# A layer norm that scales the residual in place, with ACT making the next inputs and rescaling the residual later

## The chip, the cores and the metric

The kernel runs on one core of one Trainium2 chip. The core has TensorE (PE in the profile, with its weight loads as PEld), VectorE (DVE), ScalarE (ACT), GpSimd (POOL) and SyncE (SP, which here only issues transfers). The metric is the device time of one execution in microseconds. All times are from the chip, and the profile is one execution seen by the hardware profiler.

## The reference

A trunk of two layers works on x of 512 positions by 1024 channels. Each layer has three sublayers: a half-step feed-forward network (FFN), a token mixer (Mamba-2 SSD in layer 0, differential attention in layer 1), and a second half-step FFN. Every sublayer ends in the same way, and the next one begins with a modulation:

```
y = sublayer(x * (1 + scale) + shift)
x = layer_norm(ALPHA * x + gate * y, g, b)      # mean and variance over 1024 channels
layer_norm(v) = (v - mean) * rsqrt(var + 1e-5) * g + b
```

So between two sublayers two things are made from the normalised value `n = (v - mean) * rsqrt(var + eps)`: the next sublayer's inputs `u = n*G + B`, where G and B join the norm's g, b with the next scale and shift, and the next residual `ALPHA*x = n*(ALPHA*g) + ALPHA*b`. All matrix products are float32 in the reference.

## The kernel before

**Numbers.** Each float32 operand of a product is split in a high part in fp32r and a low part, the rest. A product takes three matmuls: high by high, high by low, low by high (L162). The high part is made by ACT as a rounded copy, the low part by DVE as a subtraction (L119 and L120 for most weights, L449 and L450 for others, L149 and L150 for activations). The norm's outputs are split likewise in `uh` and `ul`.

**Layout.** Activations lie transposed, channels on the 128 partitions and the 512 positions along a row. The residual is one tile `resid` of 8 blocks (d = 0 to 7) of 128x512. Sublayers are counted n = 0 to 5: FFN, SSD, FFN, FFN, attention, FFN.

**The end of a sublayer** (`down_units`, class `LN`). The down projection is added into the residual block by block by DVE (`add_res`, L366). The last four (or six) blocks are done in two halves of 256 positions, so that the first half can be normalised while TensorE still works on the second. `stats` gets mean and variance by small matmuls, GpSimd raises the variance to the power -0.5 (L317), and matmuls with the identity spread the result over the partitions into a PSUM tile `rb`. DVE then subtracts the mean in place (L321). `normalize` does, for each half and each block d:

```
lt = res * G * rb            # DVE, L348, reads PSUM
uh = lt + B   (fp32r)        # ACT, L349
ul = (lt + B) - uh           # DVE, L350
```

and at the half's end ACT copies `rb` to an SBUF tile `rs` (L353). After both halves `residual` makes the next residual on GpSimd: for each d, `res = res * rs` (L359) and `res = res * lnag + lnab` (L360), all 512 positions at once. It is first used when the next sublayer adds to the residual.

**The start of the next sublayer.** Its first weights (tiles `wah`, `wal`) were split ahead, and its first products run on halves, so that TensorE starts with the first half of `uh` and `ul`. In the FFNs n = 2, 3 and 5 the first four of 22 tiles are plain products (gate and up, then SiLU L533, product L535). In their course DVE and ACT build sums of the input blocks (`input_forms`, L426 to L431). The remaining 18 tiles use a scheme with seven products of half size in place of eight (`seven`), whose weight sums and splits DVE and ACT make for each tile (L449, L450, L459). While a tile runs, DVE also does multiply-and-sum units of the modulation's projection (`ada_unit`, L180).

**What sets the order.** The code records operations for each engine, and a list scheduler of the language orders each engine's instructions by its own estimate of when they could run; each engine then executes its list strictly in order and waits on semaphores. Only SyncE's queue issues weight loads, into four buffers `raw`.

Of the kernel before, what the change touches and what calls it, by code (L numbers as in the profile page):

```python
# [9 lines left out]
F32 = mybir.dt.float32  # L10
# [36 lines left out]
def hybrid_trunk(tc, xT, cb, par, cst, adaw, wgu, wdn0, wdn1, wdn2, wdt, win, wso, wqk, wv, wao, dist_in, dtp, lam_in, out):  # L47
# [17 lines left out]
    def tmp(name="tmp"):  # L65
        return tp.tile([P, T], F32, tag="t", name=name)
# [193 lines left out]
    class LN:  # L260
# [63 lines left out]
        def normalize(self, a, b, rb):  # L324
            n = self.n
            if n == 5:
                for d in range(KT):
                    t = res[d][:, a:b]
                    nc.vector.scalar_tensor_tensor(
                        out=t, in0=t, scalar=pc(C_LNG + n * 8 + d), in1=rb, op0=ALU.mult, op1=ALU.mult  # L330
                    )
                    nc.scalar.activation(t, t, AF.Identity, bias=pc(C_LNB + n * 8 + d))
                    if d % 2:
                        nc.sync.dma_start(
                            out[(d - 1) * P : (d + 1) * P, a:b].rearrange("(e p) t -> p e t", e=2),
                            resid[:, d - 1 : d + 1, a:b],
                        )
                return
            if self.u is None:
                self.u = [  # L340
                    tuple(ap.tile([P, T], F32R, tag="u", name=x, bufs=2 * KT) for x in ("uh", "ul")) for _ in range(KT)
                ]
                self.rs = ap.tile([P, T], F32, tag="l", name="rs", bufs=3)
            for d in range(KT):
                G, B = lnG[n][:, d : d + 1], lnB[n][:, d : d + 1]
                t = tmp("lt")[:, a:b]
                uh, ul = self.u[d][0][:, a:b], self.u[d][1][:, a:b]
                nc.vector.scalar_tensor_tensor(out=t, in0=res[d][:, a:b], scalar=G, in1=rb, op0=ALU.mult, op1=ALU.mult)  # L348
                nc.scalar.activation(uh, t, AF.Identity, bias=B)  # L349
                nc.vector.scalar_tensor_tensor(  # L350
                    out=ul, in0=t, scalar=B, in1=uh.bitcast(F32), op0=ALU.add, op1=ALU.subtract
                )
            nc.scalar.activation(self.rs[:, a:b], rb, AF.Copy)  # L353

        def residual(self):
            n = self.n
            if n < 5:
                for d in range(KT):
                    nc.gpsimd.tensor_tensor(out=res[d], in0=res[d], in1=self.rs, op=ALU.mult)  # L359
                    nc.gpsimd.tensor_scalar(  # L360
                        out=res[d], in0=res[d], scalar1=lnag[n][:, d : d + 1],
                        scalar2=lnab[n][:, d : d + 1], op0=ALU.mult, op1=ALU.add,
                    )

    def add_res(d, pd, n, a, b):
        nc.vector.scalar_tensor_tensor(  # L366
# [135 lines left out]
    def ffn(n, stream=None, per=(0, 0), pre=None, first7=FT):  # L502
# [9 lines left out]
        for pi, nf in enumerate(FPARTS):  # L512
            hs = []
            open7 = None
            for _ in range(nf):
                if f >= first7:
                    g = seven(load(wgu[idx, f, 0]), load(wgu[idx, f, 1]), forms, hs)
                    next(g)
                    if open7 is not None:
                        next(open7, None)  # L520
                    next(g)
                    open7 = g
                    f += 1
# [12 lines left out]
                hs.append(split_act(h))  # L536
                if first7 - 4 <= f < first7:
                    making = making or input_forms(u)
                    forms.append(next(making))
                f += 1  # L540
                if f > 3 or n > 0:
                    advance(stream, per[0])

            if open7 is not None:
                next(open7, None)

            def mk(d):
# [20 lines left out]
    def ssm(n):  # L568
# [307 lines left out]
    def attention(n):  # L876
# [285 lines left out]
```

## Time and profile before

| | us |
|---|---|
| median of 3 runs | 2261.39 |
| lowest, highest | 2259.89, 2261.66 |
| the profiled execution | 2260.94 |
| its span | 2259.2 |
| PE, DVE, ACT, POOL busy | 2170.5, 1746.3, 989.0, 403.5 |
| mean granted TensorE clock | 0.988 |

The profiled execution's time is 1.7 us more than its span, which counts from the first instruction's start to the last one's end. A group's row gives the line, the engine, the operation, out<-in by tile names, the shape, the count, and then the busy time, the mean of one in ns and the idle time just before. A wait's row gives the waiting engine, tile and line, the releaser, the total in us, how many times, and the longest. A row of stretches gives the stretch, its length, the busy time and count for PE, PEld, DVE, ACT and POOL, the granted clock (1.00 is full), the share of the DMA engines and GB/s. The norms' ends lie at 380 to 400 us (n = 0), 833 to 851 (n = 1), 1209 to 1233 (n = 2), 1580 to 1603 (n = 3) and 1879 to 1900 (n = 4).

### The profile page before, as it was taken

What the parts mean: (1) busy time and instruction counts of PE and PEld (TensorE: products, weight loads), DVE (VectorE), ACT (ScalarE), POOL (GpSimd) and SP (SyncE); (2) the same over time, 40 slices, a digit from 0 to 9 for tenths busy, and PEclk for the clock granted to TensorE, in tenths of its full rate; (3) what the DMA queues carried; (4) which work ended last, traced back from release to release, by engine and by line L of the source; (5) the groups of instructions that cost most, each with busy time, mean ns of one, the idle gap of its engine ahead of it and who ended that gap; (6) DMA issues with size and microseconds to landing.
All of it is one profiled execution on the core that took longest, in us unless ns stands there. A gap on an engine that the chain in (4) does not pass through costs nothing.

```text
span 2259.2 us, 33641 instructions
## 1 busy us (share of the span) xinstructions
PE 2170.5 (96%) x13030; PEld 1866.5 (83%) x13030; DVE 1746.3 (77%) x2850; ACT 989.0 (44%) x1648; POOL 403.5 (18%) x412
## 2 busy tenths in 40 slices
PE   7999999999999988999999899999999999899998
PEld 5788889866777677898999889899877779889897
DVE  6864668656766689998888998897866679959696
ACT  4422234567656534343453334343555544425353
POOL 3000003344222335000014200003300025100003
PEclk9999999999999999999999999999999999999999
DMA  8864652564544413646442273633211111323231
GB/s 301 281 212 161 206 169 78 124 174 141 163 125 128 126 47 112 215 140 201 145 131 76 83 252 102 234 110 115 67 57 57 57 60 63 102 86 106 91 114 46
DMA packets 88545, 296.97 MB, mean 131 GB/s; under 512 B 9536, under 2 KB 12992, under 8 KB 88384
## 3 DMA queue, kind: packets, MB, share of 16 engines
q1 hardware_dynamic: 88384, 294.81, 40.9%
q8 instruction: 102, 1.67, 0.3%
q14 instruction: 59, 0.48, 0.1%
HBM read 289.53 MB, written 5.24 MB: 130 GB/s over the span
## 4 chain that ended last, share of the span: by engine, by line
PE 54%; DVE 17%; issue 5%; ACT 3%; DMA 2%; POOL 2%; POOLq 0%; ACTq 0%; DVEq 0%; SPq 0%
PE acc L162 42%; PE mid L162 5%; DVE wl L120 2%; DVE raw L459 2%; PE mid L782 2%; DVE lo L150 1%; DVE wl L450 1%; DMA raw<-in_wdn 1%; DVE ul L350 1%; DVE raw L180 1%; PE mid L931 1%; PE ln L162 1%; DVE lt L348 1%; ACT wh L119 1%; PE ln L249 1%
## 5 line engine op out<-in xcount | busy, mean ns | idle before, releaser
L162 PE MATMUL acc<-hi,wh 128*128 128x512 f32 (+1 forms) x1488 | 506.6, 341 | 20.0 <-ACT wh L449 10.0
L162 PE MATMUL acc<-hi,wl 128*128 128x512 f32 (+1 forms) x1488 | 505.9, 340 | 5.5 <-DVE wl L450 5.5
L162 PE MATMUL acc<-lo,wh 128*128 128x512 f32 (+1 forms) x1488 | 504.9, 340 | 0.0
L162 PE MATMUL acc<-uh,wh 128*128 128x512 f32 (+1 forms) x1256 | 442.6, 353 | 4.5 <-ACT px L482 4.4
L162 PE MATMUL acc<-ul,wh 128*128 128x512 f32 (+1 forms) x1256 | 439.7, 350 | 0.1
L162 PE MATMUL acc<-uh,wl 128*128 128x512 f32 (+1 forms) x1256 | 438.5, 350 | 1.3 <-DVE wl L120 1.3
L119 ACT ACTIVATE wh<-raw 128x1024 fp32r<-128x1024 f32 (+1 forms) x234 | 239.2, 1027 | 410.1 <-PE acc L162 212.1
L120 DVE TENSOR_TENSOR wl<-raw,wh 128x1024 fp32r<-128x1024 f32 (+1 forms) x234 | 288.0, 1232 | 86.5 <-ACT wh L119 77.5
L162 PEld LDWEIGHTS acc<-hi,wh 128*128 128x128 f32 x1488 | 283.5, 191 | 58.0 <-ACT wh L449 10.6
L162 PEld LDWEIGHTS acc<-hi,wl 128*128 128x128 f32 x1488 | 284.0, 191 | 37.0 <-DVE wl L450 6.3
L162 PEld LDWEIGHTS acc<-lo,wh 128*128 128x128 f32 x1488 | 283.8, 191 | 31.2 <-DVE lo L150 1.3
L162 PEld LDWEIGHTS acc<-uh,wh 128*128 128x128 f32 x1256 | 238.3, 190 | 45.1 <-issue 9.4
L162 PEld LDWEIGHTS acc<-uh,wl 128*128 128x128 f32 x1256 | 238.2, 190 | 35.9 <-issue 3.9
L162 PEld LDWEIGHTS acc<-ul,wh 128*128 128x128 f32 x1256 | 238.5, 190 | 33.8 <-issue 4.7
L449 ACT ACTIVATE wh<-raw 128x1024 fp32r<-128x1024 f32 x162 | 170.8, 1059 | 211.1 <-DVE raw L459 107.6
L180 DVE SCALAR_TENSOR_TENSOR raw<-raw,cond 128x1024 f32<-128x1024 f32 x144 | 179.5, 1254 | 52.4 <-DMA raw<-in_adaw 52.0
L450 DVE TENSOR_TENSOR wl<-raw,wh 128x1024 fp32r<-128x1024 f32 x162 | 197.0, 1220 | 28.6 <-ACT wh L449 27.7
L112 POOL TENSOR_TENSOR wal<-raw,wah 128x512 fp32r<-128x512 f32 x13 | 19.7, 1517 | 895.8 <-ACT wah L110 308.4
L366 DVE SCALAR_TENSOR_TENSOR resid<-acc,gv,resid 128x512 f32<-128x512 f32 (+1 forms) x172 | 113.0, 659 | 76.7 <-PE acc L162 76.2
L459 DVE TENSOR_TENSOR raw<-raw 128x512 f32<-128x512 f32 x216 | 150.3, 698 | 4.4
L162 PE MATMUL mid<-uh,wh 128*128 128x256 f32 (+2 forms) x332 | 94.8, 286 | 1.0 <-DVE up L491 0.9
L162 PE MATMUL mid<-uh,wl 128*128 128x256 f32 (+2 forms) x332 | 94.0, 284 | 0.6 <-DVE wl L120 0.6
(270 smaller groups left out, 3920.1 us busy)
## 6 DMA issues: line engine op xcount, KB each, us to landing
raw<-in_wgu SPq DMA_DIRECT2D x176, 512.0 KB, 3.9
raw<-in_adaw SPq DMA_DIRECT2D x144, 512.0 KB, 4.4
raw<-in_wdn SPq DMA_DIRECT2D x64, 448.0 KB, 3.5
raw<-in_win SPq DMA_DIRECT2D x40, 512.0 KB, 3.6
raw<-in_wdn SPq DMA_DIRECT2D x32, 512.0 KB, 4.6
rw<-scr SPq DMA_DIRECT2D x32, 512.0 KB, 5.6
ch<-scr SPq DMA_DIRECT2D x32, 256.0 KB, 3.6
raw<-in_wso SPq DMA_DIRECT2D x16, 512.0 KB, 3.4
```

Of the source, the lines that this page charges most:

```text
L119: nc.scalar.activation(hi[:, :n], raw, AF.Copy)
L120: nc.vector.tensor_tensor(out=lo[:, :n], in0=raw, in1=hi[:, :n].bitcast(F32), op=ALU.subtract)
L150: y = nc.vector.tensor_tensor(out=lo, in0=src, in1=hi.bitcast(F32), op=ALU.subtract)
L162: last = nc.tensor.matmul(o, lhsT=a, rhs=b, start=start and j == 0, stop=j == n - 1, skip_group_check=not start)
L180: nc.vector.scalar_tensor_tensor(out=raw, in0=raw, scalar=1.0, in1=cond, op0=ALU.mult, op1=ALU.mult, accum_out=mods[l][:, j : j + 1],)
L249: nc.tensor.matmul(o[:, j * P : (j + 1) * P], lhsT=cols[:, j : j + 1].broadcast_to([P, P]), rhs=ident, start=True, stop=True)
L348: nc.vector.scalar_tensor_tensor(out=t, in0=res[d][:, a:b], scalar=G, in1=rb, op0=ALU.mult, op1=ALU.mult)
L366: nc.vector.scalar_tensor_tensor(out=res[d][:, a:b], in0=pd[:, a:b], scalar=gvec[n][:, d : d + 1], in1=res[d][:, a:b], op0=ALU.mult, op1=A ...
L449: nc.scalar.activation(x[0], r, AF.Copy)
L450: nc.vector.tensor_tensor(out=x[1], in0=r, in1=x[0].bitcast(F32), op=ALU.subtract)
L459: nc.vector.tensor_tensor(out=o, in0=x, in1=y, op=ALU.add)
L782: nc.tensor.matmul(py[hh * 64 : (hh + 1) * 64, cc], lhsT=lhs, rhs=rhs, start=k == 0, stop=k == 2)
```

## The change

For the norms n = 0 to 4, `normalize` now multiplies the centred residual by `rb` in place on DVE, so that the residual block itself holds the normalised value. ACT makes `uh` from it with scale G and bias B, and a second time, unrounded, `lt`; DVE subtracts the two for `ul`. The tile `rs` and its copies are gone. `residual` issues nothing itself: it puts eight operations on a list `later`, each of which rescales one block (128x512) on ACT with scale and bias. They are issued by `scale_residual`: in an FFN two after each of the first four tiles, in the SSD after the first SiLUs, in the attention after the first value unit. The last norm, n = 5, is unchanged.

```diff
             if self.u is None:
                 self.u = [
                     tuple(ap.tile([P, T], F32R, tag="u", name=x, bufs=2 * KT) for x in ("uh", "ul")) for _ in range(KT)
                 ]
-                self.rs = ap.tile([P, T], F32, tag="l", name="rs", bufs=3)
             for d in range(KT):
                 G, B = lnG[n][:, d : d + 1], lnB[n][:, d : d + 1]
-                t = tmp("lt")[:, a:b]
+                z, t = res[d][:, a:b], tmp("lt")[:, a:b]
                 uh, ul = self.u[d][0][:, a:b], self.u[d][1][:, a:b]
-                nc.vector.scalar_tensor_tensor(out=t, in0=res[d][:, a:b], scalar=G, in1=rb, op0=ALU.mult, op1=ALU.mult)
-                nc.scalar.activation(uh, t, AF.Identity, bias=B)
-                nc.vector.scalar_tensor_tensor(
-                    out=ul, in0=t, scalar=B, in1=uh.bitcast(F32), op0=ALU.add, op1=ALU.subtract
+                nc.vector.tensor_tensor(out=z, in0=z, in1=rb, op=ALU.mult)
+                for o in (uh, t):
+                    nc.scalar.activation(o, z, AF.Identity, bias=B, scale=G)
+                nc.vector.tensor_tensor(out=ul, in0=t, in1=uh.bitcast(F32), op=ALU.subtract)
+
+        def residual(self):
+
+            n = self.n
+
+            def mk(d):
+                return lambda: nc.scalar.activation(
+                    res[d], res[d], AF.Identity, bias=lnab[n][:, d : d + 1], scale=lnag[n][:, d : d + 1]
                 )
-            nc.scalar.activation(self.rs[:, a:b], rb, AF.Copy)
-
-        def residual(self):
-            n = self.n
-            if n < 5:
-                for d in range(KT):
-                    nc.gpsimd.tensor_tensor(out=res[d], in0=res[d], in1=self.rs, op=ALU.mult)
-                    nc.gpsimd.tensor_scalar(
-                        out=res[d], in0=res[d], scalar1=lnag[n][:, d : d + 1],
-                        scalar2=lnab[n][:, d : d + 1], op0=ALU.mult, op1=ALU.add,
-                    )
+
+            later.extend(mk(d) for d in range(KT) if n < 5)
+
+    later = []
+
+    def scale_residual(k=KT):
+        for f in later[:k]:
+            f()
+        del later[:k]
...
                     forms.append(next(making))
                 f += 1
+                scale_residual(2 if f < 5 else KT)
                 if f > 3 or n > 0:
                     advance(stream, per[0])
...
         silu(bc + xs)
+        scale_residual()
         run(units_z(0, zs[0])[:2])
...
         unit_v(0)()
+        scale_residual()
         os_ = {}
```

**The order on DVE**, at the second half of the norm n = 1 and into the FFN n = 2. Before (L321 subtracts the mean, L112 and L120 are low parts of weights, L180 is a unit of the modulation's projection):

```order
L321 TENSOR_TENSOR resid<-resid,mid 128x256 x7
L348 SCALAR_TENSOR_TENSOR lt<-resid,lnG_2252,ln 128x256 x3
L350 SCALAR_TENSOR_TENSOR ul<-lt,lnB_2254,uh 128x256 x3
L348 SCALAR_TENSOR_TENSOR lt<-resid,lnG_2252,ln 128x256 x3
L350 SCALAR_TENSOR_TENSOR ul<-lt,lnB_2254,uh 128x256 x3
L348 SCALAR_TENSOR_TENSOR lt<-resid,lnG_2252,ln 128x256 x2
L112 TENSOR_TENSOR wal<-raw,wah 128x512
L350 SCALAR_TENSOR_TENSOR ul<-lt,lnB_2254,uh 128x256 x2
L180 SCALAR_TENSOR_TENSOR raw,mods_87<-raw,cond 128x1024
L120 TENSOR_TENSOR wl<-raw,wh 128x1024
```

The same place now:

```order
L347 TENSOR_TENSOR resid<-resid,ln 128x256 x5
L350 TENSOR_TENSOR ul<-lt,uh 128x256
L347 TENSOR_TENSOR resid<-resid,ln 128x256
L350 TENSOR_TENSOR ul<-lt,uh 128x256
L347 TENSOR_TENSOR resid<-resid,ln 128x256 x2
L350 TENSOR_TENSOR ul<-lt,uh 128x256
L112 TENSOR_TENSOR wal<-raw,wah 128x512
L350 TENSOR_TENSOR ul<-lt,uh 128x256
L180 SCALAR_TENSOR_TENSOR raw,mods_87<-raw,cond 128x1024
L350 TENSOR_TENSOR ul<-lt,uh 128x256
L120 TENSOR_TENSOR wl<-raw,wh 128x1024
L350 TENSOR_TENSOR ul<-lt,uh 128x256 x2
```

The low parts `ul` have moved back among the weight and projection work that used to follow them. At the norms n = 2 and n = 4 three low parts of weights (L120) stand between the last of them in the same way.

**The order on ACT**, at the end of the same norm and in the first tiles of the FFN n = 2. Before (L533 is a tile's SiLU, L119 a high part of weights, L149 a high part of activations):

```order
L349 ACTIVATE uh<-lt,lnB_2254 128x256 x9
L353 ACTIVATE rs<-ln 128x256
L533 ACT_TABLE_LOAD
L533 ACTIVATE sg<-acc 128x512
L119 ACTIVATE wh<-raw 128x1024
L149 ACTIVATE hi<-h 128x512
L119 ACTIVATE wh<-raw 128x1024
```

The same place now, from the last pair on (the SiLU has become L538):

```order
L349 ACTIVATE uh<-resid,lnB_2254,lnG_2252 128x256
L349 ACTIVATE lt<-resid,lnB_2254,lnG_2252 128x256
L357 ACTIVATE resid<-resid,lnab_2259,lnag_2257 128x512 x3
L538 ACT_TABLE_LOAD
L538 ACTIVATE sg<-acc 128x512
L357 ACTIVATE resid<-resid,lnab_2259,lnag_2257 128x512
L119 ACTIVATE wh<-raw 128x1024
L149 ACTIVATE hi<-h 128x512
```

Each of the sixteen `uh` is now followed by its `lt`, three of the eight residual blocks stand ahead of the first SiLU, and the other five among the splits that follow.

**The order on POOL**, behind the second power of the norm n = 1. Before:

```order
L317 TENSOR_TENSOR rr<-vr,mhalf 128x2
L359 TENSOR_TENSOR resid<-resid,rs 128x512 x2
L360 TENSOR_SCALAR resid<-resid,lnag_2257,lnab_2259 128x512 x2
L359 TENSOR_TENSOR resid<-resid,rs 128x512 x2
L360 TENSOR_SCALAR resid<-resid,lnag_2257,lnab_2259 128x512 x2
```

Now the next thing GpSimd does there belongs to the end of the FFN n = 2:

```order
L317 TENSOR_TENSOR rr<-vr,mhalf 128x2
L112 TENSOR_TENSOR wal<-raw,wah 128x512 x2
L277 TENSOR_TENSOR resid<-resid,m_10724 128x512 x2
```

The sixteen residual instructions are gone from its list, as they are at the other four norms. The order of the weight loads on SP's queue is the same in both programs, but for one small load at the attention's start.

More of the change, by code (lines that the diff above doesn't have):

```diff
@@ L342, in normalize @@
                 ]
-                self.rs = ap.tile([P, T], F32, tag="l", name="rs", bufs=3)
             for d in range(KT):
                 G, B = lnG[n][:, d : d + 1], lnB[n][:, d : d + 1]
-                t = tmp("lt")[:, a:b]
+                z, t = res[d][:, a:b], tmp("lt")[:, a:b]
                 uh, ul = self.u[d][0][:, a:b], self.u[d][1][:, a:b]
-                nc.vector.scalar_tensor_tensor(out=t, in0=res[d][:, a:b], scalar=G, in1=rb, op0=ALU.mult, op1=ALU.mult)
-                nc.scalar.activation(uh, t, AF.Identity, bias=B)
-                nc.vector.scalar_tensor_tensor(
-                    out=ul, in0=t, scalar=B, in1=uh.bitcast(F32), op0=ALU.add, op1=ALU.subtract
-                )
-            nc.scalar.activation(self.rs[:, a:b], rb, AF.Copy)
+                nc.vector.tensor_tensor(out=z, in0=z, in1=rb, op=ALU.mult)
+                for o in (uh, t):
+                    nc.scalar.activation(o, z, AF.Identity, bias=B, scale=G)
+                nc.vector.tensor_tensor(out=ul, in0=t, in1=uh.bitcast(F32), op=ALU.subtract)
         def residual(self):
             n = self.n
-            if n < 5:
-                for d in range(KT):
-                    nc.gpsimd.tensor_tensor(out=res[d], in0=res[d], in1=self.rs, op=ALU.mult)
-                    nc.gpsimd.tensor_scalar(
-                        out=res[d], in0=res[d], scalar1=lnag[n][:, d : d + 1],
-                        scalar2=lnab[n][:, d : d + 1], op0=ALU.mult, op1=ALU.add,
-                    )
+            def mk(d):
+                return lambda: nc.scalar.activation(
+                    res[d], res[d], AF.Identity, bias=lnab[n][:, d : d + 1], scale=lnag[n][:, d : d + 1]
+                )
+            later.extend(mk(d) for d in range(KT) if n < 5)
[4 more added lines that the diff above has]
+        del later[:k]
     def add_res(d, pd, n, a, b):
```

## The prediction

> **What bounds the kernel now.** I read the page first, then TensorE's waits at each of the five boundaries that the change touches, then what every engine did in the stretches ahead of those waits, and last DVE's groups in one of them.
>
> ```profile
> PE 2170.5 (96%) x13030; PEld 1866.5 (83%) x13030; DVE 1746.3 (77%) x2850; ACT 989.0 (44%) x1648; POOL 403.5 (18%) x412
> ```
>
> TensorE is busy 96% of the span, so a change off its path pays only where TensorE stands still or runs slowly. Its waits from the norm n = 1 to the start of the seven-product tiles (834 to 900 us):
>
> ```profile
> PE acc L162 <- ACT wh L449: 6.5, 1, 6.5
> PE acc L162 <- ACT uh L349: 1.1, 2, 0.7
> PE acc L162 <- DVE wl L450: 1.0, 1, 1.0
> PE mid L162 <- DVE wl L120: 0.6, 1, 0.6
> PE acc L162 <- DVE wl L120: 0.5, 1, 0.5
> ```
>
> The same for n = 2 (1210 to 1285 us), for n = 3 (1593 to 1630 us) and, its three longest, for n = 4 (1880 to 1945 us). At n = 0 (380 to 445 us) the longest is the last row here.
>
> ```profile
> PE acc L162 <- ACT px L482: 2.9, 1, 2.9
> PE acc L162 <- DVE wl L450: 2.3, 1, 2.3
> PE acc L162 <- ACT wh L449: 1.6, 1, 1.6
> ```
>
> ```profile
> PE ln L953 <- DVE p L945: 1.0, 1, 1.0
> PE acc L162 <- DVE ul L350: 0.8, 1, 0.8
> ```
>
> ```profile
> PE acc L162 <- DVE wl L450: 2.2, 1, 2.2
> PE acc L162 <- ACT wh L449: 1.8, 1, 1.8
> PE acc L162 <- ACT px L482: 1.5, 1, 1.5
> ```
>
> ```profile
> PE ln L627 <- DVE E L613: 0.4, 1, 0.4
> ```
>
> At the three FFNs the long waits are all for weight splits of the first seven-product tile. Two stretches of each boundary: first the one in which GpSimd rescales the residual, then the one in which TensorE waits:
>
> ```profile
> core 0: us, PE busy (x) PEld busy (x) DVE busy (x) ACT busy (x) POOL busy (x), PEclk, DMA share, GB/s
> 850.00:885.00 35.00, 33.91 (x239) 31.39 (x238) 35.00 (x41) 13.21 (x20) 33.71 (x16) 1.00 0.47 151
> 892.00:899.00 7.00, 4.55 (x20) 4.25 (x21) 7.00 (x12) 2.06 (x4) 0.00 (x0) 0.51 0.46 152
> 1230.00:1258.00 28.00, 27.85 (x213) 26.73 (x213) 27.85 (x32) 7.32 (x12) 27.49 (x16) 1.00 0.28 95
> 1271.00:1281.00 10.00, 7.13 (x33) 6.83 (x33) 9.53 (x15) 5.10 (x8) 0.00 (x0) 0.50 0.46 151
> 1896.00:1927.00 31.00, 30.16 (x216) 28.22 (x215) 31.00 (x33) 12.12 (x18) 30.03 (x16) 1.00 0.26 85
> 1933.00:1940.00 7.00, 4.14 (x18) 3.57 (x17) 6.90 (x12) 3.43 (x6) 0.00 (x0) 0.51 0.24 77
> ```
>
> DVE is busy without a break (35.00 of 35 us) while ACT is not half busy. So behind "ACT wh" and "ACT px" too stands DVE, which makes what ACT waits for. The clock is at half speed exactly where TensorE has stood still: each stall is paid twice.
>
> DVE is late because of GpSimd. Its groups from 850.6 to 884.3 us, the sixteen residual instructions' stretch at n = 1:
>
> ```profile
> L120 DVE TENSOR_TENSOR wl<-raw,wh 128x1024 fp32r<-128x1024 f32 x5 | 8.7, 1734 | 0.0
> L180 DVE SCALAR_TENSOR_TENSOR raw<-raw,cond 128x1024 f32<-128x1024 f32 x4 | 6.4, 1594 | 0.0
> L150 DVE TENSOR_TENSOR lo<-fb,hi 128x512 fp32r<-128x512 f32 x2 | 2.9, 1435 | 0.0
> L150 DVE TENSOR_TENSOR lo<-ft,hi 128x512 fp32r<-128x512 f32 x2 | 2.5, 1228 | 0.0
> L426 DVE TENSOR_TENSOR ft<-uh,ul 128x512 f32<-128x512 f32 x2 | 2.4, 1224 | 0.0
> L430 DVE TENSOR_TENSOR fb<-fb,ft 128x256 f32<-128x256 f32 x2 | 1.9, 958 | 0.0
> L429 DVE TENSOR_TENSOR ft<-ft,fb 128x256 f32<-128x256 f32 x2 | 1.9, 958 | 0.0
> L428 DVE TENSOR_TENSOR ft<-ft 128x256 f32<-128x256 f32 x2 | 1.7, 829 | 0.0
> L426 DVE TENSOR_TENSOR fb<-uh,ul 128x512 f32<-128x512 f32 x2 | 1.4, 681 | 0.0
> ...
> L450 DVE TENSOR_TENSOR wl<-raw,wh 128x1024 fp32r<-128x1024 f32 x1 | 1.2, 1214 | 0.0
> ...
> L431 DVE TENSOR_TENSOR fb<-fb 128x256 f32<-128x256 f32 x2 | 0.8, 414 | 0.0
> ```
>
> The last three rows show what the shapes cost undisturbed: 1.21 us for 1024 columns, 0.68 for 512, 0.41 for 256. Against them the rows above lost: L120 5 x 0.52 = 2.6; L180 4 x 0.38 = 1.5; the three at 512 2 x (0.76 + 0.55 + 0.54) = 3.7; the three at 256 2 x (0.55 + 0.55 + 0.42) = 3.0. That is 10.8 us, or 0.32 us for each us that GpSimd was busy. By this ratio n = 2 lost 27.5 x 0.32 = 8.8 and n = 4 30.0 x 0.32 = 9.6 us (estimates).
>
> **The change part by part.** *GpSimd's residual goes.* DVE is earlier by 10.8, 8.8 and 9.6 us at the FFN boundaries. How much of that TensorE gets is capped by what it loses there now:
>
> - n = 1: 6.5 + 1.0 + 0.6 + 0.5, and the longer wait for `uh`, 0.7 (it is for the second half, which DVE starts late), 9.3 us. From 892 to 899 it was busy 4.55 us at clock 0.51, worth 2.3 at full speed: 2.2 more. Sum 11.5.
> - n = 2: 2.9 + 2.3 + 1.6 = 6.8; from 1271 to 1281 7.13 us at 0.50, so 3.6 more. Sum 10.4.
> - n = 4: 2.2 + 1.8 + 1.5 = 5.5; from 1933 to 1940 4.14 us at 0.51, 2.0 more. Sum 7.5.
> - n = 3: 0.8 + 1.0 = 1.8 (the late `ul`, and the first scores). n = 0: nothing to win.
>
> *DVE's two operations of a slice become plain two-operand ones.*
>
> ```profile
> L350 DVE SCALAR_TENSOR_TENSOR ul<-lt,lnB,uh x80: 467/480/1528, 383.4 to 1898.2; 128x256 fp32r<-128x256 f32 x80
> ```
>
> From 0.48 (median) to L431's 0.41 us: 32 x 0.07 = 2.2 us of DVE at each norm. With it DVE's lead is 13.0, 11.0 and 11.8 us against the 11.5, 10.4 and 7.5 that TensorE could use. So the stalls can go entirely, 31.2 us with n = 3, but at n = 1 and 2 with only 0.6 to 1.5 us to spare.
>
> *ACT gets more.* It makes 32 pieces of 256 columns at each norm instead of 16, with two pointers (scale and bias) instead of one, and then 8 blocks of 512.
>
> ```profile
> L349 ACT ACTIVATE uh<-lt,lnB x80: 492/498/515, 382.9 to 1895.8; 128x256 fp32r<-128x256 f32 x80
> ```
>
> ```profile
> L1037 ACT ACTIVATE uf<-resid,sh,sc x8: 799/802/803, 10.1 to 54.1; 128x512 f32<-128x512 f32 x8
> ```
>
> ```profile
> L149 ACT ACTIVATE hi<-sg 128x512 fp32r<-128x512 f32 x54 | 33.9, 628 | 36.0 <-DVE sg L498 36.0
> ```
>
> ```profile
> 844.62 1.31 ACT L349 ACTIVATE uh<-lt,lnB 128x256 fp32r<-128x256 f32 x3 [3.59 <-DVE lt L348]
> ```
>
> L1037 is the new form itself, at 512 columns: 0.80 us, 0.17 more than L149's without pointers, so 0.09 for a pointer and 0.59 for the new piece of 256. Three of L349 in a row take 1.31, so each adds (1.31 - 0.50) / 2 = 0.41, 0.09 less than its length; the new pieces then add 0.50 each, a block of the residual 0.71. At each norm: 32 x 0.50 + 8 x 0.71 = 21.7 us, where 16 x 0.41 and two copies `rs` (some 0.3 each, an estimate) were 7.2. ACT had 35.00 - 13.21 = 21.8 us free in the 35 us after n = 1 alone, so the 14.5 us more fit. What shows of it:
>
> - A slice is ready after 2 x 0.50 = 1.00 us of ACT; before, DVE's two operations paced it, at about 2 x 0.40. At the FFNs TensorE uses a slice in nine matmuls (three weight tiles are split ahead), and the stretches above have 0.13 to 0.14 us for a matmul (33.91 us for 239, 27.85 for 213), so about 1.2 us: ACT keeps pace. The attention has two tiles, six matmuls, 0.8 us; there up to 8 x 0.2 = 1.6 us of the 1.8 could be lost again. I count none of it, since the second half starts earlier, but keep it for the bound. DVE does not idle meanwhile, since the scheduler moved weight splits between its `ul`.
> - The first `ul` waits for one more ACT piece, 0.5 us, in the four places where TensorE waits for a norm now (`uh` twice at n = 1, once at n = 4, `ul` at n = 3): 4 x 0.5 = 2.0 us lost.
> - Blocks of the residual stand in ACT's list ahead of a SiLU or of the splits L119 and L149; each can hold these up by 0.71 us. DVE has some lead for that; I take one hold-up at each of three FFN starts, 2.1 us. At n = 0 eight blocks, 5.7 us, come among the SiLUs of the SSD's first group, where no wait of TensorE is near: nothing, at most 5.7.
>
> The residual itself is due only when the next sublayer's down projection adds to it, after the first tiles of an FFN or later; it is ready sooner than it was. No buffer gets scarcer.
>
> **The sum.** 11.5 + 10.4 + 7.5 + 1.8 - 2.0 - 2.1 = 27.1 us. The profiled execution took 2260.94, 0.45 below the median of the runs, 2261.39. 2260.9 - 27.1 = 2233.8; with the median's offset 2234.3. Small waits that I have not counted (0.7 and 0.8 us at n = 4, among others) lean the other way, so I say 2233. Bounds: if everything listed goes and no cost shows, and the SSD gains as much as n = 3, 2261 - 33 - 4 = 2224; if half of the relief arrives, 2247.
>
> *The page's rule on the clock.* The row 1271 to 1281 has half clock where the longest single wait is 2.9 us. The Trainium skill (TensorE: Matmul & The Clock Gate, "What's actually happening") says the clock falls after an idle window of about 3.4 us. Read for single waits, only n = 1 would give its clock back, and the sum would be 5.6 us smaller; the row differs, and the sum above goes by the row.
>
> **The rivals.** *Half the relief (2247).* With DVE earlier, the splits wait next for their loads or for ACT's in-order list: from 1271 to 1281 the DMA engines work at 0.46 and ACT is busy 5.10 of 10 us. Against it: from 850 to 885 DVE never waited for a load, and the loads wait for DVE to free their buffers. The price is half the 29.4 us of the three FFNs: 14.7 us back, plus nothing new.
>
> *No change (2261).* DVE's stretching might be its own, not GpSimd's; then only the 2.2 us at each norm remain, and the ACT costs of 4.1 us eat most of it: 3 x 2.2 - 4.1 = 2.5 us faster, in the noise. Against it: the same form costs 0.68 and 1.22 within one stretch, which data or shape cannot explain.
>
> *ACT takes DVE's place (2278, slower).* If ACT's list, not DVE, decides at the first tiles of the three FFNs, then the eight blocks of 0.71 (5.7 us) delay the splits whose lateness TensorE already feels there, with the stalls of today still in place: 3 x 5.7 = 17 us more. It decides from the point where ACT has no idle time left between the norm and the first seven-product tile; 13.21 of 35 us says it is far from that. The Trainium skill speaks for this rival (ScalarE: Activation LUTs, "Rules for kernel authors": adds and multiplies belong on VectorE); the rows here show DVE as the one that is full.
>
> **How the numbers follow.** Forecast, most or all of the stalls gone: 0.70. Half: 0.15. No change: 0.07. ACT: 0.08. The likeliest time is 2233. The range, 8 in 10, takes the lower bound 2224 with a little for a shuffled order, and reaches to the half case: 2221 to 2249. A measurement of this kernel can tell about 0.2%, 4.5 us, from no change: faster 0.85, same 0.07, slower 0.08.
>
> **What would show it.** L120, L150, L426 to L431 keep to 1.21, 0.68 and 0.41 us throughout the first tiles of the FFNs, and GpSimd is idle there. The waits on weight splits at the seven-product start fall from 9, 7 and 6 us to under 2 each, and the granted clock stays at 1.00 there. DVE's busy time falls by some 45 us in all (norms 11, stretching 34), ACT's rises by about 70, GpSimd's falls by 130. The new pieces take 0.59, the blocks 0.80 us. I am wrong if DVE is still full up to the first seven-product tile, or if TensorE waits for `lt`, `ul` or a SiLU behind the blocks for several us at a boundary.

## The result and the profile after

The kernel after took 2224.32 us (median of 4 runs, 2221.89 to 2227.95), the kernel before 2260.64 us beside it (2255.46 to 2261.66). The ratio is 0.9845, 95% interval 0.9825 to 0.9866: 36.3 us faster, where 28 were forecast. In a later comparison on one chip the same kernel took 2223.53 us, ratio 0.9839 (0.9822 to 0.9856). The profiled execution after took 2227.95 us, the longest of its four, with a span of 2226.2, 33.0 less than before's.

First the busy times of the page after:

```profile
PE 2161.8 (97%) x13030; PEld 1862.6 (84%) x13030; DVE 1697.3 (76%) x2850; ACT 1055.2 (47%) x1758; POOL 273.4 (12%) x332
```

DVE has 49.0 us less, ACT 66.2 more, GpSimd 130.1 less. TensorE's waits from the norm n = 1 into the FFN (834 to 905 us; at n = 2 and n = 4 the same view is the second and third fence, 1195 to 1285 and 1850 to 1945 us). The weight sums and splits of the seven-product tiles now stand in L454 and L455, which were L449 and L450:

```profile
PE acc L162 <- DVE wl L455: 1.1, 2, 0.9
PE acc L162 <- ACT uh L349: 0.8, 2, 0.4
PE acc L162 <- DVE ul L350: 0.5, 1, 0.5
PE mid L162 <- ACT hi L149: 0.3, 1, 0.3
```

```profile
PE ln L249 <- POOL rr L317: 0.2, 1, 0.2
```

```profile
PE acc L162 <- ACT uh L349: 1.2, 1, 1.2
PE ln L249 <- POOL rr L317: 0.3, 1, 0.3
```

At n = 1 the longest wait fell from 6.5 to 0.9 us; at n = 2 and n = 4, where the longest were 2.9 and 2.2, none on a weight sum or split is left. The stretches that answer to those of before, each time the one after the norm and then the one with the first seven-product tile:

```profile
849.00:884.00 35.00, 34.98 (x258) 33.20 (x257) 32.24 (x58) 27.52 (x44) 0.00 (x0) 1.00 0.46 151
884.00:898.00 14.00, 13.51 (x99) 12.52 (x98) 14.00 (x23) 6.64 (x10) 0.00 (x0) 1.00 0.29 87
1213.00:1241.00 28.00, 27.91 (x233) 27.91 (x234) 26.50 (x56) 22.11 (x38) 0.04 (x1) 1.00 0.29 95
1241.00:1262.00 21.00, 21.00 (x132) 18.84 (x131) 20.12 (x33) 10.47 (x14) 0.00 (x0) 1.00 0.30 93
1865.00:1896.00 31.00, 30.97 (x255) 30.59 (x254) 28.82 (x56) 25.89 (x43) 0.71 (x1) 1.00 0.27 86
1896.00:1912.00 16.00, 16.00 (x95) 14.15 (x95) 15.93 (x27) 7.75 (x13) 0.00 (x0) 1.00 0.21 67
```

TensorE stands still for at most 0.5 us of a stretch. The granted clock is 1.00 in all six, where before it was 0.51, 0.50 and 0.51 around the waits. GpSimd is idle but for at most 0.7 us, and DVE has 1.5 to 2.8 us free in the stretch after each norm. Some of DVE's groups from 850 to 885 us (rows between them are left out):

```profile
L120 DVE TENSOR_TENSOR wl<-raw,wh 128x1024 fp32r<-128x1024 f32 x5 | 6.1, 1219 | 0.0
L180 DVE SCALAR_TENSOR_TENSOR raw<-raw,cond 128x1024 f32<-128x1024 f32 x4 | 4.9, 1221 | 2.6 <-DMA raw<-in_adaw 2.6
L150 DVE TENSOR_TENSOR lo<-ft,hi 128x512 fp32r<-128x512 f32 x3 | 2.1, 684 | 0.0
L431 DVE TENSOR_TENSOR ft<-uh,ul 128x512 f32<-128x512 f32 x3 | 2.0, 683 | 0.0
L434 DVE TENSOR_TENSOR ft<-ft,fb 128x256 f32<-128x256 f32 x3 | 1.2, 416 | 0.0
```

L120 went from 1734 to 1219 ns, the 512-column forms from 1228 to 684, the 256-column forms from 958 to 416. DVE now waits for a load (2.6 us), which it did not in this stretch before. The new operations, with shortest, median and longest:

```profile
L349 ACT ACTIVATE uh<-resid,lnB,lnG x80: 583/587/602, 383.1 to 1875.1; 128x256 fp32r<-128x256 f32 x80
L350 DVE TENSOR_TENSOR ul<-lt,uh x80: 408/419/642, 384.8 to 1876.5; 128x256 fp32r<-128x256 f32 x80
L357 ACT ACTIVATE resid<-resid,lnab,lnag x40: 797/804/813, 403.4 to 1886.4; 128x512 f32<-128x512 f32 x40
```

To see where the 33 us went, each matmul of the three-matmul products (L162, counted from the first) is looked up in both traces, and the start in the trace of before is subtracted from the start in the trace of after. The table gives by how much this shift changes between two places, in the time of before. Beside it stand the prediction's terms and costs for the same place:

| place (us of before) | what lies there | shift, us | forecast |
|---|---|---|---|
| 380 to 460 | n = 0, SSD start | +3.4 | 0 |
| 460 to 833 | SSD | -1.0 | 0 |
| 833 to 920 | n = 1, FFN start | -9.4 | -11.5 + 1.0 + 0.7 = -9.8 |
| 920 to 1209 | FFN | -1.8 | 0 |
| 1209 to 1310 | n = 2, FFN start | -10.9 | -10.4 + 0.7 = -9.7 |
| 1580 to 1645 | n = 3, attention start | -2.7 | -1.8 + 0.5 = -1.3 |
| 1879 to 1956 | n = 4, FFN start | -10.4 | -7.5 + 0.5 + 0.7 = -6.3 |
| all others | | 0.2 or less each | 0 |

The +3.4 is a stretch at half clock that this execution had and before's did not:

```profile
425.00:429.00 4.00, 3.57 (x25) 2.96 (x23) 2.32 (x5) 0.42 (x1) 0.00 (x0) 1.00 0.29 93
429.00:436.00 7.00, 7.00 (x24) 5.76 (x24) 1.38 (x3) 4.11 (x9) 0.00 (x0) 0.51 0.29 70
```

Both executions have the same wait of 0.4 us ahead of it (on `E`, DVE, in the SSD's start), and before kept 1.00. In the profile of the later repeat of the kernel after, the clock of this stretch is 0.76 and the whole shift is -38.8 us. Of the 6.2 us between the two profiles of one kernel, this stretch gives 1.9; 1.8 lie at 920 to 1209 us and 2.3 at 1310 to 1580 us, for reasons that stay open. At the four norms n = 1 to 4 the two profiles agree within 0.8 us. So one profile tells the boundaries well, and the sum over the whole span only to some 6 us.

### The profile page after: what moved, and what is told of

It is laid out like the page before. It is cut to its first block, busy times and chain, and to the rows that moved or that the text cites. A ratio compares the mean times of both kernels' runs of the same rounds, so it can differ in the third digit from the quotient of the medians.

```text
span 2226.2 us, 33653 instructions
## 1 busy us (share of the span) xinstructions
PE 2161.8 (97%) x13030; PEld 1862.6 (84%) x13030; DVE 1697.3 (76%) x2850; ACT 1055.2 (47%) x1758; POOL 273.4 (12%) x332
## 4 chain that ended last, share of the span: by engine, by line
PE 48%; DVE 9%; issue 4%; ACT 3%; DMA 2%; POOL 1%; POOLq 0%; ACTq 0%; DVEq 0%; SPq 0%
PE acc L162 38%; PE mid L162 6%; DVE wl L120 1%; DMA raw<-in_wdn 1%; PE mid L938 1%; DVE raw L464 1%; PE ln L162 1%; DVE wl L455 1%; DVE raw L180 1%; DVE lo L150 1%; PE ln L249 1%; DMA raw<-in_adaw 1%; ACT wh L119 1%; DVE resid L277 1%; DVE resid L371 0%
## 5 line engine op out<-in xcount | busy, mean ns | idle before, releaser
L162 PE MATMUL acc<-hi,wh 128*128 128x512 f32 (+1 forms) x1488 | 506.0, 341 | 9.8 <-DVE resid L371 6.7
L162 PE MATMUL acc<-hi,wl 128*128 128x512 f32 (+1 forms) x1488 | 505.9, 340 | 1.1 <-DVE wl L455 1.1
L162 PE MATMUL acc<-lo,wh 128*128 128x512 f32 (+1 forms) x1488 | 504.9, 339 | 0.0
L162 PE MATMUL acc<-uh,wh 128*128 128x512 f32 (+1 forms) x1256 | 441.6, 352 | 0.3 <-ACT wh L119 0.3
L162 PE MATMUL acc<-ul,wh 128*128 128x512 f32 (+1 forms) x1256 | 439.5, 350 | 0.2 <-DVE ul L1047 0.2
L162 PE MATMUL acc<-uh,wl 128*128 128x512 f32 (+1 forms) x1256 | 438.2, 349 | 0.8 <-DVE wl L120 0.8
L119 ACT ACTIVATE wh<-raw 128x1024 fp32r<-128x1024 f32 (+1 forms) x234 | 238.6, 1025 | 392.3 <-PE acc L162 199.1
L120 DVE TENSOR_TENSOR wl<-raw,wh 128x1024 fp32r<-128x1024 f32 (+1 forms) x234 | 281.2, 1202 | 81.1 <-ACT wh L119 71.3
L162 PEld LDWEIGHTS acc<-hi,wh 128*128 128x128 f32 x1488 | 283.8, 191 | 46.2 <-DVE resid L371 6.5
L162 PEld LDWEIGHTS acc<-hi,wl 128*128 128x128 f32 x1488 | 284.1, 191 | 32.2 <-DVE wl L455 1.5
L162 PEld LDWEIGHTS acc<-lo,wh 128*128 128x128 f32 x1488 | 283.9, 191 | 31.0 <-DVE lo L150 1.0
L162 PEld LDWEIGHTS acc<-uh,wh 128*128 128x128 f32 x1256 | 237.4, 189 | 40.2 <-issue 9.2
L454 ACT ACTIVATE wh<-raw 128x1024 fp32r<-128x1024 f32 x162 | 170.8, 1059 | 207.5 <-DVE raw L464 105.2
L162 PEld LDWEIGHTS acc<-uh,wl 128*128 128x128 f32 x1256 | 237.6, 189 | 35.0 <-issue 3.9
L162 PEld LDWEIGHTS acc<-ul,wh 128*128 128x128 f32 x1256 | 237.8, 189 | 33.7 <-issue 4.4
L180 DVE SCALAR_TENSOR_TENSOR raw<-raw,cond 128x1024 f32<-128x1024 f32 x144 | 176.9, 1235 | 55.8 <-DMA raw<-in_adaw 55.4
L455 DVE TENSOR_TENSOR wl<-raw,wh 128x1024 fp32r<-128x1024 f32 x162 | 196.9, 1219 | 27.1 <-ACT wh L454 26.1
L112 POOL TENSOR_TENSOR wal<-raw,wah 128x512 fp32r<-128x512 f32 x13 | 19.7, 1517 | 951.7 <-ACT wah L110 655.5
L162 PE MATMUL mid<-uh,wh 128*128 128x256 f32 (+2 forms) x332 | 94.7, 286 | 0.9 <-DVE up L496 0.9
L162 PE MATMUL mid<-uh,wl 128*128 128x256 f32 (+2 forms) x332 | 93.9, 283 | 0.0
```

The costliest lines, as they stand in the source:

```text
L119: nc.scalar.activation(hi[:, :n], raw, AF.Copy)
L120: nc.vector.tensor_tensor(out=lo[:, :n], in0=raw, in1=hi[:, :n].bitcast(F32), op=ALU.subtract)
L162: last = nc.tensor.matmul(o, lhsT=a, rhs=b, start=start and j == 0, stop=j == n - 1, skip_group_check=not start)
L180: nc.vector.scalar_tensor_tensor(out=raw, in0=raw, scalar=1.0, in1=cond, op0=ALU.mult, op1=ALU.mult, accum_out=mods[l][:, j : j + 1],)
L454: nc.scalar.activation(x[0], r, AF.Copy)
L455: nc.vector.tensor_tensor(out=x[1], in0=r, in1=x[0].bitcast(F32), op=ALU.subtract)
```

## The experiments

All medians below stand beside runs of the kernel before on the same chip (2259.75 to 2260.64 us). Two theories to begin with: GpSimd's residual stretched DVE's operations (the prediction's), or DVE's own cheaper operations and the new order made the gain.

**GpSimd's residual left out of the kernel before.** The body of `residual` is left out, so the residual stays unscaled; in short:

```diff
         def residual(self):
+            return
```

> The kernel before, without GpSimd's sixteen residual operations at each norm (the residual stays unscaled: this part of the computation is left out). DVE's normalising operations stay the old ones of 0.48 us, ACT gets nothing new. Theory (GpSimd's operations stretch DVE's, and DVE is late at the first seven-product tile): the stalls of n = 1, 2, 3 and 4, 11.5 + 10.4 + 1.8 + 7.5 = 31 us by the prediction's terms, go almost entirely, 2224 to 2234 us; L120 takes 1.22 us throughout 850 to 885 us. Rival (DVE's own operations, or the order of the work, made the gain): 2255 us or more, the wait of 6.5 us for a weight split stays.

2221.99 us, ratio 0.9833 (0.9818 to 0.9848). The waits of TensorE from 834 to 905 us, and two stretches:

```profile
PE acc L162 <- ACT uh L349: 0.7, 1, 0.7
```

```profile
849.00:884.00 35.00, 35.00 (x251) 32.98 (x250) 35.00 (x58) 18.87 (x26) 0.00 (x0) 1.00 0.50 166
884.00:898.00 14.00, 13.89 (x114) 13.46 (x113) 13.22 (x24) 6.19 (x10) 0.00 (x0) 1.00 0.29 91
```

The whole gain is there with the old normalising operations (`ul` still takes 480 ns in the median). It is there in the old order too: in this trace DVE's 2850 and ACT's 1648 instructions come in the same order as in the trace of the kernel before, so the order cannot have made it. DVE is as full as before, 35.00 of 35, yet TensorE no longer waits: being full is not being late. The rival, DVE's own operations or the new order, falls.

**The residual left out of the kernel after.** Nothing is put on the list `later`:

```diff
-            later.extend(mk(d) for d in range(KT) if n < 5)
```

> The kernel after, without ACT's eight residual blocks at each norm (that part of the computation is left out). The prediction charged them 2.1 us, one hold-up of 0.71 us at each of three FFN starts, and up to 5.7 us at n = 0: 2222 us if the charge was right, at the lowest 2216. If ACT has room for them, as its 27.34 of 35 us after n = 1 suggests: no difference, 2220 to 2228 us.

2222.09 us (0.9835, 0.9819 to 0.985). That is the time of the run above: the new and the old normalisation cost the same once GpSimd is still. ACT's blocks cost at most the 1.4 to 2.2 us by which the kernel after is longer (2223.53 and 2224.32), a difference inside the spread.

**GpSimd's work put back on scratch.** Into the kernel after, behind `later.extend`, with `dA`, `dB`, `dC` tiles of 128x512 (shortened):

```diff
+            for d in range(KT):          # for n < 5
+                i0 = self.u[0][1] if d == 0 else dA
+                nc.gpsimd.tensor_tensor(out=dC, in0=i0, in1=dB, op=ALU.mult)
+                nc.gpsimd.tensor_scalar(out=dC, in0=dA, scalar1=lnag.., scalar2=lnab..)
```

> The kernel after, with sixteen GpSimd operations of the old forms (eight products of two SBUF tiles, eight scalings of one) added at each of the five norms, on scratch tiles that nothing reads; the first waits for the norm's input tile 0, as the old ones did. Theory: DVE's two-input operations are stretched again to 1.7 to 2.3 us and 70 to 100% of the gain is lost, less what DVE's shorter operations keep: 2245 to 2262 us. Rival (the gain came from DVE's shorter operations and the new order): 2220 to 2229 us, as the kernel after.

2249.48 us (0.9955, 0.9939 to 0.9972): 25 of the 36 us are gone, with a result that nothing reads, and with DVE's and ACT's instructions in the order of the kernel after. By place, against the kernel after, 10.1 us are lost at n = 1, 7.8 at n = 2, 0.6 at n = 3 and 8.7 at n = 4, where the change had won 9.4, 10.9, 2.7 and 10.4. So the work on scratch brings back all of the loss at n = 1 and most at n = 2 and n = 4. Three of DVE's groups while GpSimd works at n = 1 (845 to 874 us; this kernel's L123, L353 and L442 are L120, L350 and L431 of after):

```profile
L123 DVE TENSOR_TENSOR wl<-raw,wh 128x1024 fp32r<-128x1024 f32 x3 | 5.2, 1717 | 0.0
L353 DVE TENSOR_TENSOR ul<-lt,uh 128x256 fp32r<-128x256 f32 x7 | 5.0, 729 | 0.2 <-ACT lt L352 0.2
L442 DVE TENSOR_TENSOR ft<-uh,ul 128x512 f32<-128x512 f32 x2 | 2.5, 1239 | 0.0
```

The splits and sums are stretched as before the change (1734, 1224). The stretching also falls on `ul` now, since the scratch work may start while these are still being made.

**GpSimd busy without reading.** In place of the scratch operations, one product and then forty memsets at each norm n < 5 (shortened):

```diff
+            nc.gpsimd.tensor_tensor(out=dC, in0=self.u[0][1], in1=dB, op=ALU.mult)
+            for _ in range(40):
+                nc.gpsimd.memset(dC, 1.0)
```

> The kernel after, with forty GpSimd memsets of 128x512 on a scratch tile added at each norm, behind one product that waits for the norm's input: some 30 us of GpSimd at the same place, which writes SBUF and reads nothing. If DVE is stretched only by GpSimd operations that read SBUF: as the kernel after, 2220 to 2229 us, L120 at 1.22 us. If any GpSimd work on SBUF does it: 2245 to 2262 us, as with the scratch products.

2224.6 us (0.9852, 0.9831 to 0.9872), the time of the kernel after, again in its order on DVE and ACT. The memsets, and DVE's splits and multiply-and-sum units from 846 to 870 us:

```profile
L368 POOL MEMSET dC<- 128x512 f32 x200 | 105.5, 527 | 11.4
```

```profile
L123 DVE TENSOR_TENSOR wl<-raw,wh 128x1024 fp32r<-128x1024 f32 x5 | 6.1, 1227 | 0.0
L183 DVE SCALAR_TENSOR_TENSOR raw<-raw,cond 128x1024 f32<-128x1024 f32 x3 | 3.7, 1219 | 2.2 <-DMA raw<-in_adaw 2.2
```

The memsets alone kept GpSimd busy for 105.5 us, and these operations of DVE keep their length. So GpSimd's being busy, or its writing of SBUF, is not what stretches them; what the scratch operations have beyond that is the reading of SBUF. The Trainium skill says so (SBUF — State Buffer, "Who interferes with whom"): a DVE instruction with two SBUF inputs contends with a GpSimd instruction that reads SBUF, not with one that only writes it. The memsets agree.

**The residual's second half on GpSimd, ACT not used.** The normalised value already lies in the residual, so only the scaling is left, eight operations of one SBUF input at each norm. Two places: at once, and at the kernel's later places (both edits in one, shortened).

```diff
-                return lambda: nc.scalar.activation(
-                    res[d], res[d], AF.Identity, bias=lnab.., scale=lnag..)
+                return lambda: nc.gpsimd.tensor_scalar(
+                    out=res[d], in0=res[d], scalar1=lnag.., scalar2=lnab.., op0=ALU.mult, op1=ALU.add)
-            later.extend(mk(d) for d in range(KT) if n < 5)     # only in the run "at once"
+            for d in range(KT): mk(d)()
```

> The kernel after, with the eight scalings of the residual on GpSimd instead of ACT, given out at once after the norm: half of GpSimd's old operations, those with one SBUF input, and the same results. By the scratch run, which lost 25 us at three FFN starts for 24 us of GpSimd at each (0.35 us for each us), eight scalings of about 1.9 us should lose 3 x 15 x 0.35 = 16 us: 2240 us, range 2234 to 2246. If only GpSimd's products of two tiles stretch DVE's operations, or if DVE's shorter operations leave room for the half: 2222 to 2228 us.

> The same eight GpSimd scalings, at the changed kernel's later places (two after each of the first tiles of an FFN). If what counts is how much GpSimd does before the first seven-product tile, the later place lies still inside that stretch and DVE is still full: 2234 to 2246 us, as when given out at once. If the later place alone heals: 2222 to 2228 us.

2225.28 us (0.9843, 0.9828 to 0.9857) at once, 2227.36 (0.9855, 0.984 to 0.9869) later. Both miss the forecast of 2240: nearly nothing is lost. GpSimd's scalings in the first of the two, then DVE's splits beside them (847 to 863 us):

```profile
L357 POOL TENSOR_SCALAR resid<-resid,lnag,lnab 128x512 f32<-128x512 f32 x40 | 61.1, 1541 | 18.8 <-ACT lt L349 18.8
```

```profile
L120 DVE TENSOR_TENSOR wl<-raw,wh 128x1024 fp32r<-128x1024 f32 x3 | 4.4, 1490 | 0.0
L350 DVE TENSOR_TENSOR ul<-lt,uh 128x256 fp32r<-128x256 f32 x8 | 3.7, 478 | 0.1
```

They are stretched, but little: 1.7 us of DVE in 15.6 us of GpSimd. Both runs have DVE's and ACT's instructions in the same order as the kernel after without its residual (2222.09), so that run is the closest to compare with: at once, the scalings lose 1.3 us at n = 1, 0.4 at n = 2 and 0.4 at n = 4 against it. So the 0.35 us of time for each us of GpSimd, by which I forecast, does not carry over from a mixture to scalings alone. The next theory: GpSimd's products of two tiles do most of the harm.

**Products alone, scalings alone, on scratch.** The scratch loop with the eight products only, and with sixteen scalings only.

> The kernel after, with eight GpSimd products of two SBUF tiles on scratch at each norm and no scalings: half of the instructions of the run that lost 25 us. In the kernel before, DVE instructions that overlap only products lost 15.5 us in 33.1 us of overlap (0.47 for each), those that overlap only scalings 5.3 in 58.6 (0.09). If the products are what stretches DVE: eight of 1.6 to 1.9 us cost DVE 6 to 7 us at each FFN start; between the run that lost 1.8 us of DVE and nothing of the time, and the one that lost 10.4 and 25 us, that gives some 14 us: 2238, range 2232 to 2246 us. If both kinds count alike and DVE has room for half: 2222 to 2228 us.

> The kernel after, with sixteen GpSimd scalings of one SBUF tile on scratch at each norm and no products: as many instructions and as long (some 24 us or more) as in the run that lost 25 us. If the products are what stretches DVE: 24 to 30 us of scalings cost DVE only 2 to 3.5 us at a norm, 2222 to 2231 us. If GpSimd's busy time counts whatever it reads: 2240 to 2252 us.

2254.18 us (0.9977, 0.9964 to 0.999) with the products, 2233.18 (0.9883, 0.9864 to 0.9901) with the scalings. Eight products lose 30 us, more than the sixteen mixed operations and twice what I had said (2238, at most 2246). Sixteen scalings, over twice as long on GpSimd, lose 9 to 10, a little more than I had said. Both runs keep the order of the kernel after on DVE and ACT. With the products, TensorE's waits from 840 to 900 us, and DVE's groups from 849 to 864 us:

```profile
PE acc L165 <- DVE ul L353: 5.8, 5, 1.9
PE acc L165 <- ACT uh L352: 0.4, 1, 0.4
```

```profile
L353 DVE TENSOR_TENSOR ul<-lt,uh 128x256 fp32r<-128x256 f32 x7 | 7.2, 1037 | 0.2 <-ACT lt L352 0.2
L123 DVE TENSOR_TENSOR wl<-raw,wh 128x1024 fp32r<-128x1024 f32 x1 | 2.3, 2305 | 0.0
```

With the scalings, three of DVE's groups from 844 to 872 us:

```profile
L123 DVE TENSOR_TENSOR wl<-raw,wh 128x1024 fp32r<-128x1024 f32 x4 | 6.1, 1526 | 0.0
L353 DVE TENSOR_TENSOR ul<-lt,uh 128x256 fp32r<-128x256 f32 x8 | 4.3, 548 | 0.2 <-ACT lt L352 0.2
L446 DVE TENSOR_TENSOR fb<-fb 128x256 f32<-128x256 f32 x2 | 1.7, 830 | 0.0
```

The price of one collision differs, not only their number. Put together at n = 1, "DVE lost" is the excess of DVE's instructions over the lower quartile of their form, summed over GpSimd's stretch where it is above 0.15 us. "Time lost" is the change of the shift against the kernel after, between 833 and 915 us of the kernel after (for before, the n = 1 row of the first table):

| run | GpSimd there | its stretch, us | DVE lost, us | time lost, us | median, us |
|---|---|---|---|---|---|
| before | 8 products, 8 scalings | 33.7 | 10.8 | 9.4 | 2260.6 |
| scratch | 8 products, 8 scalings | 28.7 | 10.5 | 10.1 | 2249.5 |
| scratch | 8 products | 13.1 | 7.6 | 6.5 | 2254.2 |
| scratch | 16 scalings | 27.4 | 4.4 | 4.6 | 2233.2 |
| at once | 8 scalings | 15.6 | 1.7 | 0.0 | 2225.3 |
| memsets | one product, 40 memsets | 23.3 | 0.8 | 0.3 | 2224.6 |
| after | nothing | 0 | 0 | 0 | 2224.3 |

A product costs DVE 0.58 us for each us of its own, a scaling 0.11 to 0.16. At this boundary the time follows DVE's loss closely once that is above some 2 us; below, it costs little or nothing (the 1.7 us at once cost 1.3 against the run of the same order above). The whole kernel's time does not go by n = 1 alone: the eight products lose less there than the mixture, but more at n = 0 (5.7 against 1.1 us), n = 3 (4.9 against 0.6) and n = 4 (10.7 against 8.7). At n = 0 and n = 3 the products cost DVE 7.7 us each, the mixture 3.7 and 5.0. At all three TensorE waits longer for `ul`: 2.5, 2.7 and 4.8 us, against 0.6, 0.2 and 1.6 with the mixture. The scratch products may therefore be dearer than the same products were in the kernel before, whose first started together with the last two `ul`; that was not run apart.

**ACT's blocks at once, and the blocks on DVE.**

```diff
-            later.extend(mk(d) for d in range(KT) if n < 5)
+            for d in range(KT): mk(d)()        # ACT, at once after the norm
```

> The kernel after, with ACT's eight residual blocks given out at once after the norm instead of a few tiles later: 8 x 0.71 = 5.7 us of ACT in one piece, ahead of SiLUs and splits. If ACT has room (27.34 of 35 us busy after n = 1, 20.08 of 30 after n = 2): 2222 to 2228 us. If a piece of 5.7 us in ACT's list holds up what TensorE needs at the three FFN starts and at n = 0: up to 4 x 5.7 = 23 us, 2235 to 2247 us.

2234.17 us (0.9887, 0.9871 to 0.9904), 10 us more than the kernel after. ACT's list at n = 1 holds the eight blocks in one piece, ahead of a SiLU and the next splits; TensorE's longest wait from 855 to 900 us, and the stretch in which it stands:

```profile
850.65 5.74 ACT L357 ACTIVATE resid<-resid,lnab,lnag 128x512 f32<-128x512 f32 x8
856.41 1.28 ACT L540 ACT_TABLE_LOAD   x1
857.70 0.60 ACT L540 ACTIVATE sg<-acc 128x512 f32<-128x512 f32 x1
```

```profile
PE mid L162 <- DVE wl L120: 5.0, 1, 5.0
```

```profile
864.00:869.00 5.00, 0.09 (x1) 0.09 (x1) 5.00 (x10) 2.41 (x4) 0.00 (x0) 0.62 0.00 0
869.00:876.00 7.00, 7.00 (x47) 7.00 (x48) 5.00 (x6) 0.90 (x1) 0.00 (x0) 0.78 0.73 236
```

A wait for one split, 5.0 us, and the clock that goes with it: 8.6 us are lost at n = 1, 1.1 at n = 4, nothing at n = 2. But the edit moved more than ACT's blocks, since the scheduler made another list for DVE too. The product `h` behind the first SiLU and the next low part of a weight on DVE, first in this run, then in the kernel after:

```profile
858.33 0.69 DVE L542 TENSOR_TENSOR h<-sg,acc 128x512 f32<-128x512 f32 x1 [1.79 <-ACT sg L540]
867.64 1.22 DVE L120 TENSOR_TENSOR wl<-raw,wh 128x1024 fp32r<-128x1024 f32 x1
```

```profile
860.08 0.68 DVE L540 TENSOR_TENSOR h<-sg,acc 128x512 f32<-128x512 f32 x1
862.22 1.22 DVE L120 TENSOR_TENSOR wl<-raw,wh 128x1024 fp32r<-128x1024 f32 x1
```

From `h` on, 19 operations (sums and splits of activations) stand ahead of that low part here, 4 in the kernel after. ACT had made the high parts by 863.1 us, and DVE worked without a pause from 858.3 to 867.6. So most of the 5.0 us is DVE's new order. What the piece of 5.74 us itself shows is DVE's wait of 1.8 us for the SiLU, and TensorE's waits for high parts, 1.4 us in all. The two effects were not run apart, so what the place of the blocks alone costs on ACT is not shown. On GpSimd, where at once and later have one order on DVE and ACT, the place makes no difference that can be told from the spread (2225.28 and 2227.36). The other engine, with `nc.vector.tensor_scalar` in place of `nc.scalar.activation` at the later places, run twice, the second time beside the kernel after:

> The kernel after, with the residual's blocks on DVE instead of ACT, at the same later places. A DVE operation with one SBUF input and two pointers took 0.48 us at 512 columns (L944 of the kernel before), so 8 x 0.48 = 3.8 us at each norm. DVE idled 2.6 us of 35 after n = 1, 1.4 of 30 after n = 2, 1.8 of 31 after n = 4; so some 1 to 2.5 us are missing at each of the three: 2226 to 2232 us. If DVE had room for it: 2222 to 2226 us.

> The kernel after itself once more, for the comparison with the next run on one chip: 2221 to 2228 us.

> The kernel after with the residual's blocks on DVE instead of ACT, once more, to settle whether it beats the kernel after, on the same chip. The first time it took 2221.2 us against 2224.3 on another day's chip, a difference that those runs cannot tell from none. If DVE's 0.48 us a block takes less out of the critical stretch than ACT's 0.71: 2219 to 2223 us. If the two are alike: within 2 us of each other.

2221.15 us (0.983, 0.9815 to 0.9844) the first time, 2224.1 (0.9846, 0.9828 to 0.9865) the second, beside 2223.53 (0.9839, 0.9822 to 0.9856) for the kernel after. The two are alike; the first run's lead lies inside the spread. A block on DVE took 0.54 us, not the 0.48 that I had taken from L944, which has one pointer and not two:

```profile
L357 DVE TENSOR_SCALAR resid<-resid,lnag,lnab x40: 529/541/549, 400.5 to 1890.6; 128x512 f32<-128x512 f32 x40
```

So who rescales the residual does not matter among GpSimd, DVE and ACT, once the product with `rs` is gone. No version with the whole computation beats the kernel after by more than the spread.

## Why the prediction was right, and where not

**The cause: right, and shown.** GpSimd's residual stretched DVE, DVE's late splits stopped TensorE, and each stop cost clock besides. Taking GpSimd's operations away alone, with DVE's and ACT's order unchanged, gives all of the gain; putting them back on scratch takes 25 of 36 us away, again with the order unchanged. The expected marks are all there: DVE -49 us (45 said), ACT +66 (70), GpSimd -130 (130), pieces of 0.587 and blocks of 0.804 us (0.59, 0.80), clock 1.00.

**The size: 28 said, 36 measured.** The terms that were off:

- *n = 4 was mis-sized*: 6.3 net, measured 10.4. I took three waits, 5.5 us, and left 0.7 (`hi`) and 0.8 (`ul`) out, with another 0.3 for `sc`; all went. That is 1.8, the costs that did not come are 1.2, and about 1 us is not accounted for.
- *The costs, 4.1 us, hardly came.* "The first `ul` waits for one more ACT piece" showed at one place of four (0.5 us, a new wait at n = 1; the waits on `uh` are 0.8 against 1.1 at n = 1 and 1.2 against 1.1 at n = 4). The hold-ups of 0.71 us by residual blocks show in no wait of TensorE but, at most, the 0.3 us for `hi` at n = 1, and leaving the blocks out gains at most 1.4 to 2.2 us, not to be told from nothing. When the blocks come at once, DVE does wait 1.8 us for the SiLU behind them.
- *n = 2 and n = 3* gave 1.2 and 1.4 more than said. Of that, 0.7 and 0.5 are the costs that did not come, and at n = 3 another 0.3 is a wait for `sm` (L934) that I had not listed. For the rest, 0.5 and 0.6, no step is known. The 1.6 us that slower slices might have cost at n = 3 did not come: TensorE has no wait there.
- *920 to 1209 us* gave 1.8 that no step had; why stays open. *n = 0* lost 3.4 in the profiled execution, by the clock, which I had at nothing.

**"Only 0.6 to 1.5 us to spare" was wrong.** The old operations of DVE, 2.2 us dearer at each norm, reach the same time with GpSimd still, and 1.7 to 1.9 us of stretching cost at most 1.3 us at a boundary. DVE's shorter operations were part of the argument for a full relief, and they were not needed. The estimates "8.8" and "9.6" for n = 2 and n = 4, by 0.32 us for each us of GpSimd, were low: summed over the instructions, before lost 11.2 and 10.9 there. The ratio itself holds only for that mixture.

**The rivals.** *Half the relief* did not come: the waits on splits at the seven-product starts are gone except 1.1 us at n = 1; loads or ACT did not take DVE's place. *No change* is excluded by the two runs that take GpSimd's work away and put it back. *ACT takes DVE's place* did not come in the kernel after. With the blocks at once, 8.6 us are lost at one FFN start of three although ACT has idle time, but there the long wait lies mostly in DVE's order, so that run does not test the rival's condition. The rule of the Trainium skill (ScalarE: Activation LUTs, "Rules for kernel authors") that adds and multiplies belong on VectorE makes no difference here: 2221.2 and 2224.1 us on DVE, 2224.3 and 2223.5 on ACT.

## What to carry to other kernels

When the bounding engine's feeder has operations that take 1.3 to 2.3 times their usual length, look at what GpSimd does at that moment before shortening the feeder: here removing one GpSimd product for each block was worth some 32 to 39 us, whichever engine did the scaling at the later places, and shortening DVE's operations nothing that can be measured. Judge off-loaded work by what it reads, since GpSimd's two-tile products cost DVE 0.58 us for each us, one-tile scalings 0.11 to 0.16, and forty memsets next to nothing (0.8 us in 23). After moving work, read the other engines' lists again as well: giving the eight blocks out at once put 19 operations in place of 4 ahead of a split on DVE, and that kernel was 10 us slower.

## What was not expected of the hardware

- The harm is unequal by GpSimd's operation: 1.1 us for a collision with a product (a 1024-column split took 2305 ns for 1219), some 0.4 for one with a scaling (a sum of 256 columns 830 for 416). The mean loss at n = 1 is 0.58 us for each us of products and 0.11 to 0.16 for each us of scalings.
- The clock was halved from 429 to 436 us in one execution and stayed at 1.00 in another, behind the same wait of 0.4 us (0.76 in the later repeat and in the kernel before without its residual, 1.00 in the first run with the blocks on DVE). The Trainium skill (TensorE: Matmul & The Clock Gate, "What's actually happening") lets the clock fall after an idle window of about 3.4 us; this stretch does not agree, as TensorE was busy 3.57 of the 4 us ahead of it. From 427.1 us on its matmuls there are 32 columns wide (L633); whether that matters no run shows, and what decides the clock here stays open.
